# Products of zeros ahead of the first loads, and the first two weights' sums on VectorE with their late token blocks behind the next weights

## The chip, the cores and the metric

The kernel runs on one core of one Trainium2 chip. The core has a matrix engine (PE, with PEld for its weight loads), a vector engine (DVE), a scalar engine (ACT), GpSimd (POOL) and SyncE (SP), which here only issues DMA transfers. Sixteen DMA engines move data between HBM and the core's memory, SBUF; matrix products land in PSUM. The metric is the device time of one execution in microseconds. The time before is 1756.33 us, the median of three runs (1754.27 to 1756.72).

## The reference

One encoder layer for 1024 tokens of width 1024, with 16 learned meta tokens put in front. All arithmetic is float32. What the change touches is the very first step: the input projection of the normalised tokens, whose columns feed a retention branch, an attention branch and two gates.

```python
h = jnp.concatenate([meta, x], axis=1)
# per layer
u = _rmsnorm(h, norm_mix_w)
proj = u @ w_in
rq, rk, rv, rg, a_cq, a_ckv, a_kr, a_gret, a_gmla = jnp.split(proj, SPLIT_IDX, axis=-1)
y_ret = _head_group_norm(_bidir_retention(rq, rk, rv, decay_fwd, decay_bwd), gn_w)
y_ret = (silu(rg) * y_ret) @ w_ret_out
y_mla = _mla_attention(...) @ w_mla_out
h = h + (sigmoid(a_gret) * y_ret + sigmoid(a_gmla) * y_mla) @ w_o
h = h + (silu(u2 @ w_gate) * (u2 @ w_up)) @ w_down      # u2 = _rmsnorm(h, norm_ffn_w)
return _rmsnorm(h, norm_final_w)[:, N_META:]
```

## The kernel before

**Numbers in two halves.** PE multiplies operands of type float32r. A float32 tile is therefore split into a high half, a cast on ACT, and a low half, tile minus high half, on DVE (`split`, line 153; `bsplit` and `bscale`, lines 276 and 282, for token blocks, the latter with a factor per partition). Each product of two tiles is three matmuls: high by high, high by low, low by high.

**Seven products instead of eight.** A 256-column slice of a weight and the tokens are treated as 2 x 2 matrices of blocks. `seven` (line 184) loads the four blocks of a weight (a11, a21, a22, a12), forms sums of them (lines 192 to 194: s1 = a21 + a22, s2 = s1 - a11, a21 - a11, and later on line 210 s2 - a12), and returns `prod(b)`, which splits one of the seven sides and multiplies it with the token block of the same name. The names are 11, t2, t3, n1, 21, t4 and 22 (lines 30 and 31); in each of them four token blocks of 128 x 512 (q = 0 to 3) are summed, so one name is 12 matmuls. `seven_out` and `rest_out` combine the products into four output quarters; `rest_out` (line 303) takes one or more weights and goes through the names stage by stage: t2 of each, n1 of each, t3, t4, 22.

**The start** (lines 325 to 422). Products 11 and 21 of the first NP = 7 weights need no sums. For the first four weights the loop at line 356 loads x and the weight in turn (`xload`, line 328; `wfirst`, line 336: load, then split), scales and splits the token block, and multiplies what is there. Three more weights follow (line 377), then the seven banks are copied to SBUF (line 383) and the token blocks "21" are made, then the seven weights' blocks 21 (line 387) are multiplied. All these matmuls are on line 344: 7 x 2 x 12 = 168. Between them `second(q)` (line 366) loads the other token half and makes the blocks n1 and t2. Lines 399 to 408 load the meta tokens and place them in two tiles, `um` and `umd`, whose unused columns are zero (a memset on POOL). Lines 410 to 420 make the token blocks t3, then t4 and 22. Line 421 runs the five remaining names of the first two weights as one group: 2 x 5 x 12 = 120 matmuls, on line 220. Lines 657 to 665 go on with the third and fourth weight, sums of squares of the reloaded tokens (`squares`), and the value weights.

**Buffers.** Raw weights of `wfirst` and of `seven(w7, ...)` rotate through 5 buffers (`wr1`), high and low halves through 3 each (`wh1`, `wl1`). The second weight of the first group uses other pools: `wb` (3 buffers) for its raw blocks and `wf` (2 buffers) for its sums. PSUM has two pools of four banks, `pm` and `pc`; banks 0 to 3 of the start are in `pm`, 4 to 6 in `pc`. The pools `xp`, `wf` and `wb` are closed at the end of the `with` block; the rotary tables (`cosf`, `sinf`) and the reloaded tokens (`xl`) take their place in memory, so their loads wait until the old tiles have been read.

**Order.** Engines run their own queues in order and wait for each other by semaphores. The order within each queue is planned at compile time from a simulated run: an instruction that comes earlier in the program goes first where several are ready, but a later one can pass one that is not. `tc.issue_after(ins)` puts what is traced inside it behind `ins` on that engine. DMA loads and stores are issued by SP (`load` and `store`, lines 76 and 77), also in order: a transfer that waits for a buffer holds the ones behind it.

Of the kernel before, what the change touches and what calls it, by code (L numbers as in the profile page):

```python
# [11 lines left out]
AF = mybir.ActivationFunctionType  # L12
# [5 lines left out]
P = 128  # L18
# [21 lines left out]
NP = 7  # L40

# [7 lines left out]
def build(nc, tc, A, out):  # L49
# [29 lines left out]
    def f(t):  # L79
        return t.bitcast(F32)  # L80
# [4 lines left out]
    warm = mk(cp, (P, 1), "warm")  # L85
    pool.memset(warm, 0.0)
    act.activation(warm, warm, AF.Exp)
# [9 lines left out]
    load(cols, A["cols"])  # L97
# [86 lines left out]
    def seven(pools, srcs, blocks, meta=None):  # L184
        wr, ws, wh_, wl_, pm_ = pools
        nq = len(blocks)
# [5 lines left out]
        pool.tensor_add(s1, a21, a22)  # L192
        pool.tensor_sub(s2, s1, a11)  # L193
        pool.tensor_sub(a21, a21, a11)
# [3 lines left out]
        def prod(b, qs=range(nq)):  # L198
# [9 lines left out]
            if b not in w:  # L208
                if b == "22":
                    pool.tensor_sub(s2, s2, a12)  # L210
                hi, low = slot(wh_, F32R)[:, :n], slot(wl_, F32R)[:, :n]
                act.copy(hi, side[b])  # L212
                dve.tensor_sub(low, side[b], f(hi))  # L213
                w[b] = hi, low
# [40 lines left out]
    with ExitStack() as c1:  # L255
# [13 lines left out]
        umd = mk(mp, (P, 4, 48), "umd", F32R)  # L269
        places = [bta]  # L270
# [32 lines left out]
        def rest_out(group, pl):  # L303
            for prod, e, post in group:
                dve.tensor_add(e, prod("t2"), e)
            vs = [slot(pl) for _ in group]
            for (prod, e, post), v in zip(group, vs):
                dve.tensor_sub(v, e, prod("n1"))
            for (prod, e, post), v in zip(group, vs):
                dve.tensor_add(v, prod("t3"), v)  # L310
                post("22", v)
            for prod, e, post in group:
                t = slot(pl)
                dve.tensor_add(t, prod("t4"), e)
                post("21", t)
            for prod, e, post in group:
                dve.tensor_sub(e, e, prod("22"))
                post("12", e)
# [6 lines left out]
        with ExitStack() as c2:  # L325
# [9 lines left out]

            def wfirst(src, ph, plo):
                raw = slot(wr1)
                load(raw, src)
                return split(raw, ph, plo)
# [13 lines left out]

            banks = [mk(pm if i < 4 else pc, (P, 512), "mm") for i in range(NP)]
            x11, x21, wa11, es = [], [], [], []
            for i in range(4):
                x11.append(xload(2 * i, 0))
                wa11.append(wfirst(win(i)[0], wf if i == 3 else wh1, wf if i == 3 else wl1))
# [46 lines left out]
            for dst, src in ((um, xm), (umd, xd)):  # L405
                pool.memset(f(dst), 0.0)
# [3 lines left out]
            with tc.issue_after(made[0].ins), tc.issue_after(made[1].ins):  # L410
                for q in range(4):
                    dve.scalar_tensor_tensor(x12[q], x12[q], col(2 * q), x22[q], ALU.mult, ALU.subtract)
                    hi, lo = U[q]["t3"] = block("t3")
                    made[:] = act.copy(hi, x12[q]), dve.tensor_sub(lo, x12[q], f(hi))
            with tc.issue_after(made[0].ins), tc.issue_after(made[1].ins):
                for q in range(4):
                    dve.scalar_tensor_tensor(x21[q], x21[q], col(2 * q + 1), x11[q], ALU.mult, ALU.subtract)
                    U[q]["t4"] = bsplit("t4", x21[q])
                for q in range(4):
                    U[q]["22"] = bsplit("22", x22[q])  # L420
            rest_out([(seven(w7, win(0), U), es[0], rg_post(0)),
                      (seven((wb, wf, wh1, wl1, pc), win(1), U), es[1], rg_post(1))], cr)
# [1146 lines left out]
```

## Time and profile before

| | us |
|---|---|
| median of three runs | 1756.33 |
| the profiled execution | 1753.05 |
| its span (first to last instruction) | 1751.1 |
| busy in the first 100 us: PE, DVE, ACT, POOL | 89.44, 81.62, 56.66, 38.94 |
| granted TensorE clock over the span, as a share of full speed | 0.991 |

The profile is of one execution. A row of a timeline has the start and the length in microseconds from the span's start, the engine, the line of the kernel, the operation, what it writes and reads by the program's names, shapes and count; in brackets stands how long the engine was idle before and which instruction released it. Rows of SPq are the issuing of a transfer, not the transfer. A row of the windows has the stretch, then its length, then the busy time (and the number of instructions) of PE, PEld, DVE, ACT and POOL, the granted PE clock, the share of time in which the 16 DMA engines were busy, and the rate in GB/s. Matmuls overlap, so their distance is read from the starts, not from their lengths. A few matmul records can be missing.

### The profile page before, as it was taken

To read this page: it belongs to the slowest core of one execution; us is meant where nothing else is said; L and a number is where in the kernel's file an instruction comes from. 1 tells how busy PE (TensorE), PEld (TensorE's weight loads), DVE (VectorE), ACT (ScalarE), POOL (GpSimd) and SP (SyncE) were. 2 spreads that over 40 slices of the span, in tenths; PEclk is the share of its full clock that TensorE was granted. 3 is DMA by queue.
4 is the path that set the end of the run, shared out by engine and by line. 5 is a ranking of instruction groups with operands and counts; after the bars stand their busy time and mean duration, and the time that the engine had idled before them with its cause. 6 is when DMAs were issued, how large, how long until landed. Compare 5 with 4: busy or idle time off the path is not lost. (4 is left out here: it accounts for less than half of the span.)

```text
span 1751.1 us, 26268 instructions
## 1 busy us (share of the span) xinstructions
PE 1698.3 (97%) x8644; PEld 1427.5 (82%) x8644; DVE 1346.8 (77%) x2461; ACT 852.2 (49%) x1597; POOL 763.6 (44%) x585
## 2 busy tenths in 40 slices
PE   8999999999999999999999999999999999999998
PEld 6787677888887778999898888788888888788787
DVE  7846778888789876888888768776778887866775
ACT  7426566344424624778787346433333333522335
POOL 2450267575653421324322501566676666523431
PEclk9999999999999999999999999999999999999999
DMA  7876924566546875111122844233344445876612
GB/s 261 290 250 207 296 85 131 164 211 212 193 150 226 254 280 178 30 45 30 30 64 69 272 150 162 80 108 115 129 142 144 139 138 167 273 269 226 231 61 97
DMA packets 169913, 287.15 MB, mean 164 GB/s; under 512 B 20841, under 2 KB 46882, under 8 KB 169778
## 3 DMA queue, kind: packets, MB, share of 16 engines
q1 hardware_dynamic: 168626, 284.44, 48.8%
q8 instruction: 68, 1.11, 0.3%
q10 hardware_dynamic: 1152, 1.05, 0.2%
q14 instruction: 67, 0.55, 0.1%
HBM read 193.28 MB, written 92.06 MB: 163 GB/s over the span
## 5 line engine op out<-in xcount | busy, mean ns | idle before, releaser
L220 PE MATMUL mm<-slot,slot 128*128 128x512 f32 x2604 | 595.0, 390 | 3.6 <-DVE slot L213 1.9
L220 PEld LDWEIGHTS mm<-slot,slot 128*128 128x128 f32 x2604 | 487.3, 188 | 110.2 <-DVE slot L213 4.1
L212 ACT CAST slot<-slot 128x512 fp32r<-128x512 f32 (+1 forms) x385 | 226.8, 596 | 432.2 <-PE mm L220 339.5
L213 DVE TENSOR_TENSOR slot<-slot,slot 128x512 fp32r<-128x512 f32 (+1 forms) x385 | 350.2, 912 | 67.8 <-ACT slot L212 66.9
L192 POOL TENSOR_TENSOR slot<-slot,slot 128x512 f32<-128x512 f32 (+1 forms) x57 | 78.7, 1381 | 329.5 <-DMA slot<-in_w_in 116.5
L220 PE MATMUL mm<-ht,slot 128*128 128x512 f32 x552 | 184.2, 397 | 1.9 <-DVE slot L213 1.9
L220 PE MATMUL mm<-h,slot 128*128 128x512 f32 x440 | 153.2, 408 | 5.8 <-ACT slot L212 2.8
L210 POOL TENSOR_TENSOR slot<-slot,slot 128x512 f32<-128x512 f32 (+1 forms) x57 | 76.5, 1343 | 140.8 <-DVE slot L213 97.6
L155 DVE TENSOR_TENSOR slot<-slot,slot 128x512 fp32r<-128x512 f32 x123 | 97.1, 806 | 40.4 <-ACT slot L155 36.2
L220 PEld LDWEIGHTS mm<-ht,slot 128*128 128x128 f32 x552 | 103.1, 188 | 23.8 <-DVE slot L213 2.7
L155 ACT CAST slot<-slot 128x512 fp32r<-128x512 f32 x123 | 74.5, 618 | 76.7 <-POOL slot L1275 23.4
L1092 DVE TENSOR_SCALAR_CACHE_REDUCE pr<-s,sq_c 128x384 f32<-128x384 f32 (+1 forms) x192 | 103.3, 572 | 7.9 <-PE t L1110 5.3
L220 PE MATMUL mm<-lt,slot 128*128 128x512 f32 x276 | 108.6, 394 | 0.0
L220 PEld LDWEIGHTS mm<-h,slot 128*128 128x128 f32 x440 | 84.2, 193 | 26.3 <-ACT slot L212 5.3
L140 PE MATMUL mm<-slot,slot 128*128 128x512 f32 (+1 forms) x288 | 105.4, 366 | 0.0
L141 PE MATMUL mm<-slot,slot 128*128 128x512 f32 (+1 forms) x288 | 105.3, 366 | 0.0
L139 PE MATMUL mm<-slot,slot 128*128 128x512 f32 (+1 forms) x288 | 105.2, 367 | 0.0
L193 POOL TENSOR_TENSOR slot<-slot,slot 128x512 f32<-128x512 f32 (+1 forms) x57 | 83.4, 1463 | 48.6 <-DVE slot L213 42.3
L1105 DVE TENSOR_TENSOR ptl<-t,pth 128x512 fp32r<-128x512 f32 x128 | 85.7, 684 | 17.7 <-ACT pth L1104 17.2
L1136 POOL TENSOR_TENSOR oa<-oa,ob 64x256 f32<-64x256 f32 x32 | 24.0, 749 | 151.8 <-ACT ob L1135 151.8
L220 PE MATMUL mm<-l,slot 128*128 128x512 f32 x220 | 88.6, 404 | 0.0
L1104 ACT CAST pth<-t 128x512 fp32r<-128x512 f32 x128 | 71.8, 579 | 25.2 <-PE t L1102 24.8
(409 smaller groups left out, 3667.6 us busy)
## 6 DMA issues: line engine op xcount, KB each, us to landing
slot<-in_w_in SPq DMA_DIRECT2D x90, 256.0 KB
f_d<-slot SPq DMA_DIRECT2D x71, 256.0 KB
slot<-f_d SPq DMA_DIRECT2D x71, 256.0 KB
slot<-in_xT SPq DMA_DIRECT2D x48, 256.0 KB
slot<-z_d SPq DMA_DIRECT2D x44, 256.0 KB
slot<-in_w_g SPq DMA_DIRECT2D x44, 256.0 KB
slot<-in_w_u SPq DMA_DIRECT2D x44, 256.0 KB
fl_d<-slot SPq DMA_DIRECT2D x42, 256.0 KB
```

The costliest lines, as they stand in the source:

```text
L139: pe.matmul(ps, sh, mh, start=start, stop=False)
L140: pe.matmul(ps, sh, ml, start=False, stop=False)
L141: pe.matmul(ps, sl, mh, start=False, stop=stop)
L155: split.done = act.copy(hi, t), dve.tensor_sub(lo, t, f(hi))
L192: pool.tensor_add(s1, a21, a22)
L193: pool.tensor_sub(s2, s1, a11)
L210: pool.tensor_sub(s2, s2, a12)
L212: act.copy(hi, side[b])
L213: dve.tensor_sub(low, side[b], f(hi))
L220: pe.matmul(ps, sw[:, ks], sx, start=begins and q == qs[0] and i == 0, stop=q == nq - 1 and i == 2, skip_group_check=True)
L1092: dve.tensor_scalar(pr[:, c], ps[:, :n], sq_c[:, qb : qb + 1], None, ALU.mult, ALU.max, accum_out=mx[:, j : j + 1])
L1105: dve.tensor_sub(pt[1][d], tp, f(pt[0])[d])
```

## The change

- Thirteen matmuls (`NIDLE`) of the zero tiles, 384 columns each, are put ahead of the first real product, into a PSUM bank that nothing reads. For this the zeroing of `um` and `umd` moves from line 406 to where the tiles are made, and from POOL to DVE.
- The table of per-channel factors (`cols`) and the first raw weight are loaded by DMAs that ACT issues. The dummy exponential (which makes ACT load its table) moves behind them.
- The two weights of the first group do their sums (six at once, two later) on DVE instead of POOL, by the new argument `adds`. Later weights stay on POOL.
- The two weights change places in the group.
- The making of t3, and of t4 and 22, moves into `rest_out`, between the t2 stage and the n1 stage. The second of them is issued behind the last split of the t2 stage: `split.done` is now also set in `prod`.

```diff
--- before.py
+++ after.py
@@ -39,6 +39,8 @@
 
 NP = 7
 
+NIDLE = 13
+
 O_AT = ((6, 1), (6, 2), (6, 3), (7, 0), (7, 1), (7, 2))
 
 
@@ -82,9 +84,6 @@
 
     cp = sb(top, "const")
     dram = sb(top, "scratch", space=DRAM)
-    warm = mk(cp, (P, 1), "warm")
-    pool.memset(warm, 0.0)
-    act.activation(warm, warm, AF.Exp)
     ident = mk(cp, (P, P), "ident")
     make_identity(nc, ident)
     ones = mk(cp, (P, 1), "ones")
@@ -94,7 +93,9 @@
     gneps_c = mk(cp, (P, 1), "gneps")
     pool.memset(gneps_c, GN_EPS)
     cols = mk(cp, (P, NCOL), "cols")
-    load(cols, A["cols"])
+    nc.scalar.dma_start(cols, A["cols"])
+    warm = mk(cp, (P, 1), "warm")
+    pool.memset(warm, 0.0)
     rstd = mk(cp, (P, NB + 1), "rstd")
     rst2 = mk(cp, (P, NB + 1), "rst2")
     sq_c = mk(cp, (P, NB + 1), "sq_c")
@@ -181,17 +182,18 @@
 
 
 
-    def seven(pools, srcs, blocks, meta=None):
+    def seven(pools, srcs, blocks, meta=None, adds=None):
         wr, ws, wh_, wl_, pm_ = pools
+        adds = adds or pool
         nq = len(blocks)
         n = nq * P
         a11, a21, a22, a12 = [slot(wr)[:, :n] for _ in range(4)]
         for i, t in enumerate((a11, a21, a22, a12)):
             load(t, srcs[i])
         s1, s2 = [slot(ws)[:, :n] for _ in range(2)]
-        pool.tensor_add(s1, a21, a22)
-        pool.tensor_sub(s2, s1, a11)
-        pool.tensor_sub(a21, a21, a11)
+        adds.tensor_add(s1, a21, a22)
+        adds.tensor_sub(s2, s1, a11)
+        adds.tensor_sub(a21, a21, a11)
         side = {"11": a11, "t2": s2, "t3": a21, "n1": s1, "21": a12, "t4": a22, "22": s2}
         banks, w, begun, done = {}, {}, [], set()
 
@@ -207,10 +209,9 @@
                 return ps
             if b not in w:
                 if b == "22":
-                    pool.tensor_sub(s2, s2, a12)
+                    adds.tensor_sub(s2, s2, a12)
                 hi, low = slot(wh_, F32R)[:, :n], slot(wl_, F32R)[:, :n]
-                act.copy(hi, side[b])
-                dve.tensor_sub(low, side[b], f(hi))
+                split.done = act.copy(hi, side[b]), dve.tensor_sub(low, side[b], f(hi))
                 w[b] = hi, low
             wh, wl = w[b]
             for q in qs:
@@ -267,6 +268,8 @@
         w7 = (wr1, ws1, wh1, wl1, pm)
         um = mk(mp, (P, KT, 48), "um", F32R)
         umd = mk(mp, (P, 4, 48), "umd", F32R)
+        for t in (um, umd):
+            dve.memset(f(t), 0.0)
         places = [bta]
 
         def block(nm):
@@ -300,9 +303,12 @@
                 store(rg_d[2 * j + int(name[0]) - 1, :, half(name)], side_copy(name, t))
             return post
 
-        def rest_out(group, pl):
+        def rest_out(group, pl, late=None):
+            late = late or ()
             for prod, e, post in group:
                 dve.tensor_add(e, prod("t2"), e)
+            for make in late:
+                make()
             vs = [slot(pl) for _ in group]
             for (prod, e, post), v in zip(group, vs):
                 dve.tensor_sub(v, e, prod("n1"))
@@ -333,10 +339,13 @@
             def col(k):
                 return column(C_MIX + k)
 
+            def wraw(src, begin=load):
+                raw = slot(wr1)
+                begin(raw, src)
+                return raw
+
             def wfirst(src, ph, plo):
-                raw = slot(wr1)
-                load(raw, src)
-                return split(raw, ph, plo)
+                return split(wraw(src), ph, plo)
 
             def products(ps, w, b, q, begins):
                 ks = slice(q * P, q * P + P)
@@ -351,11 +360,20 @@
                     return rg_post(i)
                 return lambda name, t: store(g_d[2 * (i - 4) + int(name[0]) - 1, :, half(name)], side_copy(name, t))
 
+
+            idle = mk(pc, (P, 512), "mm")
+            for i in range(NIDLE):
+                pe.matmul(idle[:, : KT * 48], um.rearrange("p a b -> p (a b)")[:, :P], um.rearrange("p a b -> p (a b)"),
+                          start=True, stop=True)
             banks = [mk(pm if i < 4 else pc, (P, 512), "mm") for i in range(NP)]
             x11, x21, wa11, es = [], [], [], []
+            raw = wraw(win(0)[0], nc.scalar.dma_start)
+            act.activation(warm, warm, AF.Exp)
             for i in range(4):
                 x11.append(xload(2 * i, 0))
-                wa11.append(wfirst(win(i)[0], wf if i == 3 else wh1, wf if i == 3 else wl1))
+                if i:
+                    raw = wraw(win(i)[0])
+                wa11.append(split(raw, wf if i == 3 else wh1, wf if i == 3 else wl1))
                 U[i]["11"] = bscale("11", x11[i], col(2 * i))
                 for q in range(i):
                     products(banks[i], wa11[i], "11", q, q == 0)
@@ -403,23 +421,27 @@
             x4 = xm.rearrange("p (q a) t -> p q a t", a=2)
             dve.tensor_sub(xd, x4[:, :, 1, :], x4[:, :, 0, :])
             for dst, src in ((um, xm), (umd, xd)):
-                pool.memset(f(dst), 0.0)
                 act.copy(dst[:, :, 0:NM], src)
                 dve.tensor_sub(dst[:, :, 32:48], src, f(dst)[:, :, 0:NM])
 
-            with tc.issue_after(made[0].ins), tc.issue_after(made[1].ins):
-                for q in range(4):
-                    dve.scalar_tensor_tensor(x12[q], x12[q], col(2 * q), x22[q], ALU.mult, ALU.subtract)
-                    hi, lo = U[q]["t3"] = block("t3")
-                    made[:] = act.copy(hi, x12[q]), dve.tensor_sub(lo, x12[q], f(hi))
-            with tc.issue_after(made[0].ins), tc.issue_after(made[1].ins):
-                for q in range(4):
-                    dve.scalar_tensor_tensor(x21[q], x21[q], col(2 * q + 1), x11[q], ALU.mult, ALU.subtract)
-                    U[q]["t4"] = bsplit("t4", x21[q])
-                for q in range(4):
-                    U[q]["22"] = bsplit("22", x22[q])
-            rest_out([(seven(w7, win(0), U), es[0], rg_post(0)),
-                      (seven((wb, wf, wh1, wl1, pc), win(1), U), es[1], rg_post(1))], cr)
+
+
+            def make_t3():
+                with tc.issue_after(made[0].ins), tc.issue_after(made[1].ins):
+                    for q in range(4):
+                        dve.scalar_tensor_tensor(x12[q], x12[q], col(2 * q), x22[q], ALU.mult, ALU.subtract)
+                        U[q]["t3"] = bsplit("t3", x12[q])
+
+            def make_t4():
+                with tc.issue_after(split.done[0].ins), tc.issue_after(split.done[1].ins):
+                    for q in range(4):
+                        dve.scalar_tensor_tensor(x21[q], x21[q], col(2 * q + 1), x11[q], ALU.mult, ALU.subtract)
+                        U[q]["t4"] = bsplit("t4", x21[q])
+                    for q in range(4):
+                        U[q]["22"] = bsplit("22", x22[q])
+
+            rest_out([(seven((wb, wf, wh1, wl1, pc), win(1), U, adds=dve), es[1], rg_post(1)),
+                      (seven(w7, win(0), U, adds=dve), es[0], rg_post(0))], cr, (make_t3, make_t4))
         mf = sb(mid, "factor", 1, side="right")
 
         small, sums = sb(mid, "small", 8, side="right"), sb(mid, "sums", 2, side="right")
```

## The prediction

> **What bounds the kernel now.** I read the page's head first, then a table of busy time by stretch, then the timelines of PE, DVE, POOL and SP over the stretch where PE falls behind.
>
> ```profile
> span 1751.1 us, 26268 instructions
> PE 1698.3 (97%) x8644; PEld 1427.5 (82%) x8644; DVE 1346.8 (77%) x2461; ACT 852.2 (49%) x1597; POOL 763.6 (44%) x585
> ```
>
> PE is busy for 97% of the span, so only 53 us of idle PE can be won anywhere, plus the time in which PE runs slowly. The windows (time, then busy time and instructions of each engine, granted clock, DMA share, GB/s) say where.
>
> ```profile
> core 0: us, PE busy (x) PEld busy (x) DVE busy (x) ACT busy (x) POOL busy (x), PEclk, DMA share, GB/s
> 5.00:10.00 5.00, 4.13 (x9) 2.78 (x10) 3.73 (x6) 3.61 (x7) 0.00 (x0) 1.00 1.00 330
> 10.00:20.00 10.00, 10.00 (x45) 8.22 (x44) 7.50 (x12) 7.63 (x14) 0.00 (x0) 1.00 1.05 392
> 20.00:30.00 10.00, 10.00 (x46) 8.29 (x45) 9.71 (x11) 8.78 (x16) 4.97 (x3) 1.00 0.73 259
> 30.00:40.00 10.00, 9.65 (x43) 7.67 (x42) 10.00 (x17) 7.32 (x14) 0.00 (x0) 1.00 0.61 191
> 40.00:55.00 15.00, 10.66 (x40) 8.06 (x39) 13.83 (x18) 7.67 (x16) 6.86 (x5) 0.89 0.47 153
> 55.00:81.00 26.00, 26.00 (x117) 21.53 (x116) 22.95 (x38) 15.35 (x30) 6.81 (x6) 1.00 0.96 327
> 81.00:105.00 24.00, 24.00 (x108) 19.88 (x107) 17.50 (x18) 5.28 (x9) 23.69 (x16) 1.00 0.96 331
> 140.00:190.00 50.00, 45.45 (x201) 34.47 (x200) 33.84 (x70) 35.16 (x70) 0.00 (x0) 1.00 0.72 233
> ```
>
> From 20 to 55 us DVE is the full engine, not PE. From 55 to 105 PE never idles. The rows of PE that mark the losses (start, length, engine, line, idle before and releaser):
>
> ```profile
> 5.69 0.80 PE L344 MATMUL mm<-h,slot 128*128 128x512 f32 x1 [5.69 <-ACT slot L155]
> ...
> 7.97 0.80 PE L344 MATMUL mm<-h,slot 128*128 128x512 f32 x1 [0.18 <-ACT slot L155]
> ...
> 10.64 0.40 PE L344 MATMUL mm<-l,slot 128*128 128x512 f32 x1
> ...
> 30.86 0.39 PE L344 MATMUL mm<-l,slot 128*128 128x512 f32 x1
> 31.60 0.72 PE L344 MATMUL mm<-h,slot 128*128 128x512 f32 x2 [0.35 <-DVE slot L155]
> ...
> 42.52 0.40 PE L344 MATMUL mm<-l,slot 128*128 128x512 f32 x1
> 47.26 0.73 PE L344 MATMUL mm<-h,slot 128*128 128x512 f32 x2 [4.34 <-DVE slot L155]
> ...
> 51.43 0.44 PE L220 MATMUL mm<-lt,slot 128*128 128x512 f32 x1
> ...
> 54.45 0.62 PE L220 MATMUL mm<-ht,slot 128*128 128x512 f32 x2
> ...
> 80.74 0.39 PE L220 MATMUL mm<-ht,slot 128*128 128x512 f32 x1
> ```
>
> The first pair's five stages are 5 x 24 = 120 products; four of them run early, so 116 start from 54.45 to 80.74, one every 0.2266 us. The 168 products of L344 and these 120 would take 288 x 0.2266 = 65.3 us at that pace; they take 80.74 - 5.69 = 75.05. **9.8 us are lost**, in four places. From 5.69 to 10.64 ten products start, worth 2.27 us, in 4.95: 2.7 lost. At 31.60: 31.60 - 30.86 - 0.23 = 0.5. At 47.26: 47.26 - 42.52 - 0.23 = 4.5. After that gap eleven products start from 47.26 to 51.43, worth 2.5 us, in 4.17: 1.7 lost, and the granted clock of 40 to 55 us is 0.89. About 0.4 us is left over.
>
> DVE's rows say why PE waits at 31.60 and 47.26 (both for the low half of a weight, L155), and POOL's rows beside them why DVE is late:
>
> ```profile
> 17.37 0.68 DVE L370 TENSOR_TENSOR slot<-slot,slot 128x512 f32<-128x512 f32 x1
> ...
> 24.42 1.79 DVE L373 SCALAR_TENSOR_TENSOR slot<-slot,cols,slot 128x512 f32<-128x512 f32 x1
> 26.13 1.79 DVE L285 SCALAR_TENSOR_TENSOR ln<-slot,cols,hn 128x512 fp32r<-128x512 f32 x1
> 27.84 1.78 DVE L375 TENSOR_TENSOR lt<-slot,ht 128x512 fp32r<-128x512 f32 x1
> 29.54 0.74 DVE L373 SCALAR_TENSOR_TENSOR slot<-slot,cols,slot 128x512 f32<-128x512 f32 x1
> ...
> 35.14 2.72 DVE L412 SCALAR_TENSOR_TENSOR slot<-slot,cols,slot 128x512 f32<-128x512 f32 x4
> 37.79 0.68 DVE L155 TENSOR_TENSOR slot<-slot,slot 128x512 fp32r<-128x512 f32 x1
> 38.39 2.48 DVE L414 TENSOR_TENSOR lt<-slot,ht 128x512 fp32r<-128x512 f32 x4
> 40.80 5.81 DVE L417 SCALAR_TENSOR_TENSOR slot<-slot,cols,slot 128x512 f32<-128x512 f32 x4
> 46.53 0.68 DVE L155 TENSOR_TENSOR slot<-slot,slot 128x512 fp32r<-128x512 f32 x1
> ```
>
> ```profile
> 24.02 1.64 POOL L192 TENSOR_TENSOR slot<-slot,slot 128x512 f32<-128x512 f32 x1 [21.93 <-DVE ln L285]
> ...
> 41.41 1.29 POOL L192 TENSOR_TENSOR slot<-slot,slot 128x512 f32<-128x512 f32 x1 [12.35 <-DMA slot<-in_w_in]
> ```
>
> The thirteenth weight's low half (46.53) stands behind the four L417 of the t4 blocks, and those take 1.45 us each instead of L412's 0.68 while POOL adds.
>
> **The change part by part.** *Order and engine of the sums.* Six sums (three for each of two weights) go from POOL to DVE, and two L210 later. A two-input DVE operation on this tile takes 0.68 us, with starts 0.60 apart in a chain: 6 x 0.60 = 3.6 us added before the stages, 1.2 within them. Taken off DVE: (1.79 + 1.79 + 1.78) - (0.74 + 0.74 + 0.68) = 3.2 us at 24 to 30, and 5.81 - 2.72 = 3.1 us at 41 to 46. So DVE has about 1.5 us less to do in sum, although it gets eight more instructions. The eight t3 operations (2.72 + 2.48 = 5.2 us) may fill in as now, but the twelve of t4 and 22 (about 7.6 us at 0.60 to 0.68) stand behind the next weights' splits.
>
> Does DVE make the deadlines? In the code, from the first L370 (17.37) to the last weight's low half, 25 operations must run: four each of L285 and L373 at 0.68, and nine L155, four L370, four L375 at 0.60: 15.6 us, so 33.0. With the sums 36.6, with t3 41.8. PE without stalls starts at 5.69 - 0.45 + 0.1 = 5.34, keeps 1.4 us of its first losses (both below), and ends its 168 products at 5.34 + 1.4 + 38.1 = 44.8; its thirteenth weight starts at 39.4, its fourteenth at 42.1. t3 is last in the program among these, so the weights' halves can pass it: I cost the stalls at 31.60 and 47.26 as gone, **0.5 + 4.5**, and with the gap the slow products, **1.7**. What is late next is t4, needed 72 products, 16.3 us, after 44.8: by then DVE has t4 itself (4 x 0.68 + 4 x 0.60 = 5.1), eight weight halves and six sums off the banks (14 x 0.60 = 8.4): 13.5 of 16.3. If all of t3 were left over too, 5.2 - 2.8 = 2.4 us would be lost. I take 0.
>
> The second group's sums wait for a load that starts late:
>
> ```profile
> 38.49 0.33 SPq L190 DMA_DIRECT2D slot<-in_w_in  x1
> ```
>
> It is issued when the twelfth raw weight is released by DVE (38.39) and POOL's sum starts 2.9 us later (41.41). On DVE this wait would hold everything behind it, the t2 halves and t3 to 22, for up to 2.9 us. It costs PE nothing while DVE is that far ahead: without L412 the twelfth half is done by 33.0, the wait ends at 36, before 39.4.
>
> *Start.* The zero products need only the two memsets, now on DVE; POOL's take 0.42 and 0.26:
>
> ```profile
> 1.18 0.42 SPq L330 DMA_DIRECT2D slot<-in_xT  x1
> 1.48 0.42 POOL L406 MEMSET um<- 128x384 f32 x1
> 1.65 0.42 SPq L338 DMA_DIRECT2D slot<-in_w_in  x1
> 4.41 0.72 ACT L284 ACTIVATE h<-slot,cols 128x512 fp32r<-128x512 f32 x1 [2.18 <-DMA slot<-in_xT]
> ```
>
> So PE can start near 1.2. From 7.97 to 10.64 six products start, 0.445 apart; 13 zero products of 384 columns at that pace, scaled by 384/512, take 13 x 0.33 = 4.3 us and end near 5.5, which delays the first real one by 0 to 0.3 us (I take 0.1). If PE is at full pace by 7.97, those six take 1.36 instead of 2.67: **1.3 won**. The four products before 7.97 wait for data (1.4 us of the 2.7 stays). With `cols` on ACT's queue SP issues x at 0.73 instead of 1.18: **0.45**. Below: 0, since DMA share is already 1.00 from 5 us; above: 0.92, both issues off SP. I take 0.45, as the first transfer sets when data starts to flow. ACT issues both at 0.43 each, then loads its table: done near 3.1, before x lands near 4.0.
>
> The second queue might also add bandwidth. The row 10 to 20 us has 1.05 and 392 GB/s with one queue. The Trainium skill, "DMA: Bandwidth & Descriptors", section "Issuing engines are not separate DMA queues", says that all queues run on the same 16 engines and only issue time is saved; by it this term is 0.45 to 0.92, by the other view more. The share of 1.00 agrees with the page.
>
> **Sum** at the end of the first pair: 4.5 + 1.7 + 0.5 + 1.3 + 0.45 - 0.1 = **8.4 us** (0 to 9.8 + 0.45). Behind it PE is full to 140 us, so what it gains is kept only if its feeders come earlier too. From 55 to 105 us DMA is at 0.96 and POOL at 23.69 of 24 us after 81; and the engines' orders are planned at compile time, so every later order may shift (four products of L220 before the last weight's show such a plan). From 140 to 190 PE idles 4.55 us among waits for ACT and DVE, which may grow or shrink. I take 1.9 us given back (bounds -3 to 8.4, the nearest rows being that 4.55 and the gain itself): **6.5 us net**.
>
> The profiled execution took 1753.05 (its span 1751.1 and 1.95 around it), so 1746.5 by its own time. It lies 3.3 below the median of the runs, 1756.33; a median after it should come out 6.5 below that: **1749.8**.
>
> **The rivals.** *Given back.* POOL's order and DMA's rate between 55 and 105 don't follow: bulk loads (the reloaded tokens, the value weights) keep their time, and the third and fourth weights' sums on POOL wait as now. For: DMA 0.96, POOL full. Against: PE never waited there, so there is slack that no row measures. Net 2.5 us: 1753.8. Chance 0.2.
>
> *Slower: SP is blocked by the late blocks.* The tiles that hold the tokens' raw halves are reused by the tables and token reloads:
>
> ```profile
> 52.55 0.68 DVE L279 TENSOR_TENSOR lt<-slot,ht 128x512 fp32r<-128x512 f32 x1
> ...
> 57.36 2.33 SPq L459 DMA_DIRECT2D slot<-in_xT  x5
> ```
>
> The last 22 block is now made at 52.55 and the reload starts at 57.36. If t4 and 22 slip to just before their use (44.8 + 96 x 0.2266 = 66.6), the reload starts near 67, 9.6 us later, and on SP, whose order is fixed, the next weights' loads wait behind it. PE, though early, then waits for a DMA-bound stretch that ends up to 9.6 us later than now; how much slack it has there no row shows (0 to 9.6), so I take the middle: 4.8 us above, 1761. It decides once the last 22 block is later than about 60 us. Against: DVE should have it by 54. Chance 0.1.
>
> *The zero products do nothing for PE's pace.* Then 1.3 goes: 5.2 net, 1751.1. Chance 0.1. For it: the six products at 0.445 come 2.3 us after the first real one, so pace lags work by microseconds. The Trainium skill, "TensorE: Matmul & The Clock Gate", Part 1, has a half-rate clock until a free-running window of about 3.4 us was busy. By that rule 4.3 us of products may straddle two windows, and warmth comes 3.4 to 6.8 us after 1.2, before or near 7.97. The pace in the rows agrees, though the granted clock shows 1.00 at 5 to 10 us.
>
> **How the numbers follow.** The forecast has 0.6. About 0.2%, 3.5 us, is what a measurement of this kernel can tell from no change. Faster: 0.57 of the forecast, 0.08 of the third rival, 0.05 of the first = 0.70. Slower by as much: nearly all of the second = 0.09. Within: 0.21. The range: below, 8.4 + 3 off the median, 1745; above, the first rival with nearly all given back, 1757.
>
> **What would show it.** Right: PE's first L344 near 5.3 at 0.23 spacing from 8 us; no idle over 0.5 us and clock 1.00 from 31 to 55; L344 over by 45 to 46; the third weight's first product near 72.4 instead of 80.74; DVE's operations at 0.6 to 0.75 us before 55. Wrong: an idle PE between 45 and 72 waiting for t4 or 22; SP's L459 later than 60; waits for POOL's L193 or loads at 72 to 105; or new table loads at 140 to 190.

## Result and profile after

| | before | after |
|---|---|---|
| median, us | 1754.43 (8 runs, 1751.34 to 1756.72) | 1745.24 (8 runs, 1740.51 to 1751.19) |
| ratio of the times | | 0.9948, 95% interval 0.9932 to 0.9964 |
| profiled execution, us | 1753.05 | 1740.51 |
| its span, us | 1751.1 | 1738.7 |
| third weight's first product, us | 80.74 | 73.05 |

The changed kernel is faster by 9.2 us (interval 6.3 to 11.9). 1749.8 was predicted, with 1745 to 1757 as the range, so the median lies 0.24 above the range's lower end. The profiled execution after is the fastest of its eight; that has to be kept in mind below.

Three numbers carry the comparison. **M** is the start of the third weight's first product, where the prediction closes its sum. The **gain at M** is what happened up to the end of the first pair. The **rest**, span minus M, is everything behind it. Before: M 80.74, rest 1670.4. After: M 73.05, rest 1665.7. So 7.7 us of the profiles' 12.4 come from the first pair, and 4.7 from behind it.

The head of the page, after:

```profile
span 1738.7 us, 26295 instructions
PE 1694.5 (97%) x8657; PEld 1424.9 (82%) x8657; DVE 1349.6 (78%) x2471; ACT 851.2 (49%) x1597; POOL 746.1 (43%) x575
```

PE's busy time fell by 3.8 us, although 13 products of zeros were added; the other 8.6 of the 12.4 us were idle PE. The windows after, in the same stretches and with the same columns as before:

```profile
20.00:30.00 10.00, 10.00 (x46) 8.28 (x45) 9.90 (x17) 10.00 (x20) 0.00 (x0) 1.00 0.75 251
30.00:40.00 10.00, 10.00 (x46) 8.29 (x45) 10.00 (x17) 6.45 (x12) 0.00 (x0) 1.00 0.81 269
40.00:55.00 15.00, 14.52 (x65) 11.72 (x64) 14.54 (x26) 9.59 (x19) 0.69 (x1) 1.00 0.62 206
55.00:81.00 26.00, 26.00 (x116) 21.47 (x116) 24.13 (x37) 14.04 (x25) 8.13 (x7) 1.00 0.93 326
140.00:190.00 50.00, 45.76 (x202) 35.16 (x202) 34.52 (x59) 34.58 (x65) 1.49 (x1) 1.00 0.82 264
```

From 40 to 55 us PE is busy for 14.52 us instead of 10.66, 65 matmuls start instead of 40, and the granted clock is 1.00 instead of 0.89. DVE is as full as before, but it does 26 operations in that stretch instead of 18. From 140 to 190 us PE's idle time is 4.24 us, before 4.55.

PE's rows after (start, length, idle before and releaser in brackets):

```profile
1.32 4.46 PE L366 MATMUL mm<-um 128*128 128x384 f32 x13 [1.32 <-DVE um L272]
6.52 0.50 PE L353 MATMUL mm<-h,slot 128*128 128x512 f32 x1 [0.74 <-ACT slot L156]
...
44.83 0.39 PE L353 MATMUL mm<-h,slot 128*128 128x512 f32 x1
45.05 0.39 PE L221 MATMUL mm<-ht,slot 128*128 128x512 f32 x1
...
54.77 0.50 PE L221 MATMUL mm<-ht,slot 128*128 128x512 f32 x1 [0.48 <-ACT slot L214]
...
73.05 0.39 PE L221 MATMUL mm<-ht,slot 128*128 128x512 f32 x1
```

L353 is before's L344, L221 its L220. The gaps at 31.60 and 47.26 are gone; the 168 products of the start end at 45.05. One wait is left before M, 0.48 us at 54.77. But the first real product comes at 6.52, later than before's 5.69. ACT's rows say why:

```profile
0.73 0.42 ACTq L96 DMA_DIRECT2D cols<-in_cols  x1
...
4.34 0.72 ACT L287 ACTIVATE h<-slot,cols 128x512 fp32r<-128x512 f32 x1 [1.19 <-DMA cols<-in_cols]
5.23 0.72 ACT L287 ACTIVATE h<-slot,cols 128x512 fp32r<-128x512 f32 x1 [0.17 <-DMA slot<-in_xT]
5.86 0.60 ACT L156 CAST slot<-slot 128x512 fp32r<-128x512 f32 x1
```

The factors, now issued by ACT at 0.73, are what the first scaling waits for until 4.34. Then the plan puts the second token block's scaling (5.23) ahead of the first weight's cast (5.86), which the first product needs.

DVE's rows after:

```profile
26.66 0.69 DVE L196 TENSOR_TENSOR slot<-slot,slot 128x512 f32<-128x512 f32 x1
...
32.86 2.74 DVE L432 SCALAR_TENSOR_TENSOR slot<-slot,cols,slot 128x512 f32<-128x512 f32 x4
35.51 0.69 DVE L156 TENSOR_TENSOR slot<-slot,slot 128x512 fp32r<-128x512 f32 x1
...
39.12 0.69 DVE L156 TENSOR_TENSOR slot<-slot,slot 128x512 fp32r<-128x512 f32 x1
39.73 0.69 DVE L194 TENSOR_TENSOR slot<-slot,slot 128x512 f32<-128x512 f32 x1
...
44.07 2.73 DVE L438 SCALAR_TENSOR_TENSOR slot<-slot,cols,slot 128x512 f32<-128x512 f32 x4
...
51.74 1.89 DVE L282 TENSOR_TENSOR lt<-slot,ht 128x512 fp32r<-128x512 f32 x3
```

The last (fourteenth) weight's low half (L156) is at 39.12; before, the thirteenth's was at 46.53 and the last one at 49.54. The sums (L194 to L196) take 0.69 each. The four t4 operations (L438, before L417) stand behind the weights at 44.07 and take 2.73 instead of 5.81. The last 22 block is done by 53.6.

### The profile page after: what moved, and what is told of

It is laid out like the page before. It is cut to its first block, busy times and chain, and to the rows that moved or that the text cites. A ratio compares the mean times of both kernels' runs of the same rounds, so it can differ in the third digit from the quotient of the medians.

```text
span 1738.7 us, 26295 instructions
## 1 busy us (share of the span) xinstructions
PE 1694.5 (97%) x8657; PEld 1424.9 (82%) x8657; DVE 1349.6 (78%) x2471; ACT 851.2 (49%) x1597; POOL 746.1 (43%) x575
## 4 chain that ended last, share of the span: by engine, by line
PE 66%; DVE 9%; DMA 5%; ACT 3%; issue 2%; POOL 1%; SPq 0%; DVEq 0%; ACTq 0%; POOLq 0%
PE mm L221 42%; PE o L1153 3%; PE mm L140 3%; PE mm L141 3%; PE mm L142 3%; PE t L1124 2%; PE s L140 1%; DVE slot L156 1%; PE s L142 1%; PE s L141 1%; DMA slot<-g_d 1%; PE mm L740 1%; DVE ptl L1127 1%; DVE slot L214 1%; PE mm L765 1%
## 5 line engine op out<-in xcount | busy, mean ns | idle before, releaser
L221 PE MATMUL mm<-slot,slot 128*128 128x512 f32 x2604 | 595.4, 390 | 3.7 <-DVE slot L214 1.9
L221 PEld LDWEIGHTS mm<-slot,slot 128*128 128x128 f32 x2604 | 487.2, 188 | 110.7 <-DVE slot L214 4.4
L214 ACT CAST slot<-slot 128x512 fp32r<-128x512 f32 (+1 forms) x385 | 226.7, 596 | 424.9 <-PE mm L221 340.0
L214 DVE TENSOR_TENSOR slot<-slot,slot 128x512 fp32r<-128x512 f32 (+1 forms) x385 | 352.0, 917 | 65.2 <-ACT slot L214 64.1
L194 POOL TENSOR_TENSOR slot<-slot,slot 128x512 f32<-128x512 f32 (+1 forms) x55 | 72.7, 1323 | 346.3 <-DMA slot<-in_w_in 79.6
L221 PE MATMUL mm<-ht,slot 128*128 128x512 f32 x552 | 184.0, 396 | 2.9 <-DVE slot L214 1.9
L221 PE MATMUL mm<-h,slot 128*128 128x512 f32 x440 | 151.8, 405 | 4.3 <-DVE slot L214 2.7
L156 DVE TENSOR_TENSOR slot<-slot,slot 128x512 fp32r<-128x512 f32 x123 | 100.3, 833 | 37.1 <-ACT slot L156 33.7
L212 POOL TENSOR_TENSOR slot<-slot,slot 128x512 f32<-128x512 f32 (+1 forms) x55 | 72.3, 1314 | 128.0 <-DVE slot L214 82.0
L221 PEld LDWEIGHTS mm<-ht,slot 128*128 128x128 f32 x552 | 102.8, 188 | 25.6 <-DVE slot L214 3.0
L156 ACT CAST slot<-slot 128x512 fp32r<-128x512 f32 x123 | 74.4, 619 | 76.0 <-PE mm L590 22.4
L221 PE MATMUL mm<-lt,slot 128*128 128x512 f32 x276 | 108.5, 393 | 0.0
L221 PEld LDWEIGHTS mm<-h,slot 128*128 128x128 f32 x440 | 83.4, 191 | 24.5 <-DVE slot L214 4.8
L195 POOL TENSOR_TENSOR slot<-slot,slot 128x512 f32<-128x512 f32 (+1 forms) x55 | 81.3, 1478 | 51.7 <-DVE slot L214 46.3
L221 PE MATMUL mm<-l,slot 128*128 128x512 f32 x220 | 87.8, 400 | 0.0
```

Source lines behind the costliest of these rows:

```text
L156: split.done = act.copy(hi, t), dve.tensor_sub(lo, t, f(hi))
L194: adds.tensor_add(s1, a21, a22)
L195: adds.tensor_sub(s2, s1, a11)
L212: adds.tensor_sub(s2, s2, a12)
L214: split.done = act.copy(hi, side[b]), dve.tensor_sub(low, side[b], f(hi))
L221: pe.matmul(ps, sw[:, ks], sx, start=begins and q == qs[0] and i == 0, stop=q == nq - 1 and i == 2, skip_group_check=True)
```

## Experiments

The theory: the gain at M is the group's part of the change (sums on DVE, late token blocks), which takes DVE's slow operations and the t4 blocks out of the weights' way; the start adds its own gain, mostly by the products of zeros; what lies behind M is chance. Rivals: the later 4.7 us are a second effect of the change; the sums or the order alone do all of it; the two parts need each other. All kernels but *before_again* and *zerosalone* are made from the changed one.

**Both kernels once more.** No edit, for the size of chance.

> The changed kernel, unaltered. Milestone M is the start of the third weight's first product (80.74 us before, 73.05 after); the rest is the span less M (1670.4 before, 1665.7 after). Theory A: the change acts before M alone, the other 4.7 us of the profiled runs' difference are chance from run to run. Then M comes out at 72.5 to 73.6 and the rest anywhere from 1665 to 1673. Rival B: the change also shortens the rest; then the rest is 1665 to 1667 again and that of the kernel before 1669.5 to 1671.5.

> The kernel before, unaltered, for a second trace. Theory A: M 80.2 to 81.3, and a rest (span less M) that lies among those of the changed kernel, 1665 to 1673. Rival B: a rest of 1669.5 to 1671.5, at least 3 us above the changed kernel's.

The third weight's first product of the two, each from PE's timeline of its kernel:

```profile
73.97 0.39 PE L221 MATMUL mm<-ht,slot 128*128 128x512 f32 x1
```

```profile
81.52 0.39 PE L220 MATMUL mm<-ht,slot 128*128 128x512 f32 x1
```

The changed kernel: 1748.09 us (4 runs) beside 1755.51, ratio 0.9954 (0.9939 to 0.9968); span 1747.1, so the rest is 1673.1, against 1665.7 in its first profile. The kernel before: span 1752.0, rest 1670.5 against 1670.4. The same program's rest differs by 7.4 us from one execution to the next, so the 4.7 us behind M are no effect that needs a cause. Both new M lie a little above theory A's ranges (73.97 over 73.6, 81.52 over 81.3), which were too narrow. M repeats within 0.9 us, and is the finer measure here; from now on runs are compared by it. Each of the other kernels has one trace, so a difference in M of less than about 0.9 us can't be told from chance. Mean before: 81.13. The traces of *noswap*, *startnoswap*, *groupand* and *zerosalone* come from another chip than those of the other experiments, on which neither kernel was traced again; the nearest comparison is *noswap*, whose M (73.66) lies between the changed kernel's two.

**Without the products of zeros.** The bank, the loop and its 13 matmuls are left out.

```diff
-            idle = mk(pc, (P, 512), "mm")
-            for i in range(NIDLE):
-                pe.matmul(idle[:, : KT * 48], ...
```

> The changed kernel without its 13 products of zeros (and without the PSUM tile that they write). Theory: they bring PE to full pace by the first real product; without them the first ten products come about 0.44 us apart as before, the first real product stays near 6.5 us, and M is 0.6 to 1.6 us later than 73.05: 73.7 to 74.7. Rival: PE waits for data then anyway, so the zeros are worth nothing: M 72.8 to 73.3. Second rival: the zeros delay the first real product; M 72.2 to 72.8.

M 76.23 (1751.58 us): 2.3 to 3.2 later than the changed kernel, more than the theory allowed. The first real product came at 7.36, and the products stood 0.43 apart until past 12 us. This is pace and a later first product together; *groupand* below takes them apart.

**The first loads on SP.** `cols` and the first weight are issued by SP again, the dummy exponential comes first; the rest as changed.

```diff
-    nc.scalar.dma_start(cols, A["cols"])
+    load(cols, A["cols"])
...
+    act.activation(warm, warm, AF.Exp)
...
-            raw = wraw(win(0)[0], nc.scalar.dma_start)
-            act.activation(warm, warm, AF.Exp)
```

> The changed kernel with the factors and the first weight loaded by SP in the order of before, and the dummy exponential first again. Theory: the first real product came at 6.52 us instead of 5.69 because the factors landed at 4.34 over ACT's queue and the plan put the second token block's scaling (0.63 us) ahead of the first weight's cast on ACT; with SP's loads it comes at 5.6 to 5.9 and M is 0.5 to 1.0 us earlier than 73.05: 72.0 to 72.6. Rival, as the forecast had it: the loads on ACT's queue are worth 0.45 us and the late start has another cause; then M is 73.0 to 73.6.

The time is 1746.95, ratio 0.9951 (0.9934 to 0.9967); M 73.18, within the changed kernel's own spread. The first product did come earlier, at 5.74, but nothing of that was left at M. ACT's timeline of this kernel and then PE's show two later waits:

```profile
8.19 0.72 ACT L288 ACTIVATE h<-slot,cols 128x512 fp32r<-128x512 f32 x1 [1.16 <-DMA slot<-in_xT]
```

```profile
29.59 0.50 PE L354 MATMUL mm<-h,slot 128*128 128x512 f32 x1 [0.24 <-ACT slot L157]
```

Here the third token block is waited for until 8.19; in the changed kernel it is scaled at 7.30 without a wait (at 7.85 in *again*). So the loads on ACT's queue make the first product later and a later block earlier. By the windows of the start's products, 27 start from 5 to 12.5 us here and 25 in the changed kernel; both have 148 by 40 us. The rest of the lead went at 29.59, where PE waits for the cast of a weight on ACT (busy for 10.00 of the 10 us from 20 to 30). The range of M was the rival's, its reason (another cause of the late first product) was not: the cause was right, and cost nothing.

**Sums back on POOL.**

```diff
-            rest_out([(seven((wb, wf, wh1, wl1, pc), win(1), U, adds=dve), es[1], rg_post(1)),
-                      (seven(w7, win(0), U, adds=dve), es[0], rg_post(0))], cr, (make_t3, make_t4))
+            rest_out([(seven((wb, wf, wh1, wl1, pc), win(1), U), es[1], rg_post(1)),
+                      (seven(w7, win(0), U), es[0], rg_post(0))], cr, (make_t3, make_t4))
```

> The changed kernel with the first two weights' sums back on POOL; the late blocks stay behind the t2 weights. M is the start of the third weight's first product (73.05 and 73.97 us in the two traces of the changed kernel, 80.74 and 81.52 in those of before). Theory: the gap before the thirteenth weight was made by the order of DVE's queue, POOL's sums only lengthen single operations; DVE's operations of 1.79 us come back beside the sums, PE waits 0.3 to 1.5 us for low halves near 30 us, no gap near 42; M 73.3 to 75.5. Rival: POOL's slowing of DVE made the gap; a gap of over 3 us comes back and M is 77 to 81.

M 76.13 (1751.57 us), between the theory's range and the rival's: the sums' engine is worth 2.2 to 3.1 us beside the rest of the change. No gap comes back near 47; the wait has moved behind the start, to a weight half of the group. PE's rows with a wait after 10 us:

```profile
27.33 0.74 PE L353 MATMUL mm<-h,slot 128*128 128x512 f32 x2 [0.22 <-DVE slot L156]
...
54.61 0.73 PE L221 MATMUL mm<-hn,slot 128*128 128x512 f32 x2 [1.33 <-DVE slot L214]
...
57.82 0.74 PE L221 MATMUL mm<-hn,slot 128*128 128x512 f32 x2 [0.18 <-DVE slot L214]
```

DVE's slow operations are back too: 1.79, 1.78 and 1.77 at 23.79 to 28.9 and 4.81 for the four L438, while POOL adds.

**Token blocks ahead of the group again,** sums on DVE and places swapped as changed.

```diff
+            make_t3()
+            with tc.issue_after(made[0].ins), tc.issue_after(made[1].ins):
+                for q in range(4):
+                    dve.scalar_tensor_tensor(x21[q], x21[q], col(2 * q + 1), x11[q], ALU.mult, ALU.subtract)
+                    U[q]["t4"] = bsplit("t4", x21[q])
+                for q in range(4):
+                    U[q]["22"] = bsplit("22", x22[q])
...
-                      (seven(w7, win(0), U, adds=dve), es[0], rg_post(0))], cr, (make_t3, make_t4))
+                      (seven(w7, win(0), U, adds=dve), es[0], rg_post(0))], cr)
```

> The changed kernel with the t3, t4 and 22 blocks made ahead of the group as before; the sums stay on DVE. Theory (order of the queue): four t4 products and four of their low halves, some 5 us, stand ahead of the twelfth weight's low half, which is done near 41.3 instead of 36.2 while PE needs it near 37.1: one gap of 3 to 5 us there, with slow products after it if it is over 3.4 us; M 77 to 80. Rival (contention): without POOL's sums DVE keeps up; gap under 1.5 us, M 73 to 75.

M 77.62 (1748.53 us), in the theory's range, but with two short gaps in place of one long: the order is worth about 4 us. PE's rows:

```profile
39.92 0.50 PE L353 MATMUL mm<-h,slot 128*128 128x512 f32 x1 [1.23 <-ACT slot L156]
...
42.18 0.73 PE L353 MATMUL mm<-h,slot 128*128 128x512 f32 x2 [1.52 <-DVE slot L156]
...
66.62 0.47 PE L221 MATMUL mm<-ht,slot 128*128 128x512 f32 x1 [1.02 <-ACT mm L493]
```

Two of the three waits are for the last weights' halves behind t3 and t4, as in the kernel before but shorter, since DVE's operations take 0.69 here, and with no slow products after them. The third, for the sums of squares, may have to do with the swapped places; that wasn't tried.

**The start alone on the old group.** Sums on POOL and blocks ahead, that is the edits of the last two together; zeros and ACT's loads stay. *start_only* keeps the swapped places, *startnoswap* puts them back.

> Of the change only the start (zeros, loads on ACT's queue) and the swapped places of the two weights: sums on POOL, blocks ahead of the group. Theory: PE then waits for DVE's queue near 40 us whatever it won at the start, so the start's gain is swallowed: one gap of 6 to 9 us, M 79.5 to 82.5, as before the change. Rival (the parts add up): the start's 2 us stay, M 78.0 to 79.2.

> As start_only (sums on POOL, all token blocks ahead of the group, the changed start kept) but with the two weights in their old places. Start_only gave M 85.76, 4 to 5 us later than before. Theory (the swap is what made start_only worse than before: the second weight's sums wait for a load that comes late): M 79 to 82, that is before's 80.74 to 81.52 less at most 2. Rival (an earlier start on the old group loses its gain by itself, because DVE and POOL, not PE, set the pace from 24 us on): M 84 to 87.

*start_only*: M 85.76, 1764.18 us, worse than before and outside what either theory said. *startnoswap*: M 81.02, 1754.73 us, no different from before. So swapped places cost 4.7 us on the old group. PE's waits of *start_only* that the other doesn't have lie at 66.05, 70.08 and 74.76 (0.82, 0.99 and 2.12 us, the last for the sums of squares on ACT); why the swap brings them is not settled. With the old places the start gives nothing at all: PE is ahead until 27 us, and then waits. PE's rows of *startnoswap*:

```profile
27.28 0.73 PE L353 MATMUL mm<-h,slot 128*128 128x512 f32 x2 [0.72 <-DVE slot L156]
...
38.76 0.50 PE L353 MATMUL mm<-h,slot 128*128 128x512 f32 x1 [2.26 <-ACT slot L156]
...
41.62 1.22 PE L353 MATMUL mm<-h,slot 128*128 128x512 f32 x2 [2.13 <-DVE slot L156]
```

**The places swapped back** in the changed kernel, nothing else.

```diff
-            rest_out([(seven((wb, wf, wh1, wl1, pc), win(1), U, adds=dve), es[1], rg_post(1)),
-                      (seven(w7, win(0), U, adds=dve), es[0], rg_post(0))], cr, (make_t3, make_t4))
+            rest_out([(seven(w7, win(0), U, adds=dve), es[0], rg_post(0)),
+                      (seven((wb, wf, wh1, wl1, pc), win(1), U, adds=dve), es[1], rg_post(1))], cr, (make_t3, make_t4))
```

> The changed kernel with only the first pair's two weights put back into their old places (the one with the 5-buffer pool first). M is the start of the third weight's first product; the changed kernel has shown 73.05 and 73.97. Theory (the swap does nothing, since both weights' sums are ready long before their use): M 73.0 to 74.2, DVE's sums in starts 0.60 apart, no idle PE over 0.7 us between 31 and 55. Rival (the swap is what lets the late token blocks fit, because the weight with its own buffers can be loaded first): M 75 or more, with idle PE between 40 and 60 that waits for a sum or a weight half of the first pair.

M 73.66 (1748.35 us), between the changed kernel's two. With the sums on DVE and the blocks late, the swap does nothing.

**The group's part alone.** *sp_loads* without the products of zeros: the start is the old one.

> The group's part of the change alone: sums on DVE, late token blocks, swapped places; no products of zeros, cols and first weight loaded by SP, dummy exponential first. Theory (the start is worth what no_zeros lost, 2.3 to 3.2 us, and the loads on ACT's queue nothing): M 75.3 to 77, PE's slow spacing of 0.43 until past 10 us, time 0.997 to 1.000 of before. Rival (what no_zeros lost came from the ACT-queue loads left without their cover, so that the group alone gives nearly everything): M 73 to 74.5, time 0.994 to 0.996 of before.

M 75.18; 1750.56 us (10 runs) beside 1757.66, ratio 0.9958 (0.9945 to 0.9970). M lies 0.1 below the theory's range and the ratio in the rival's; the intervals of the times can't tell 1.7 us, so M decides: the group alone gives 81.13 - 75.18 = 5.95 us. The four traces with both the zeros and the group's part (73.05 and 73.97 of the changed kernel, 73.18 of *sp_loads*, 73.66 of *noswap*) have a mean M of 73.47: the start adds 1.7. Of what *no_zeros* lost, 76.23 - 75.18 = 1.05 would belong to ACT's loads without their cover (first product at 7.36 there, at 5.90 here), which is hardly more than two executions differ by.

**The zeros alone,** added to the kernel before.

```diff
+        for t in (um, umd):
+            dve.memset(f(t), 0.0)
...
+            idle = mk(pc, (P, 512), "mm")
+            for i in range(13):
+                pe.matmul(idle[:, : KT * 48], ...
...
-                pool.memset(f(dst), 0.0)
```

> Before with only the 13 products of zeros added (the two tiles are zeroed on DVE for it). Before showed M 80.74 and 81.52. Theory (the pace gained at the start is swallowed by the stretch from 24 to 47 us, in which DVE is the full engine): M 80.2 to 82, with a gap of 4 us or more near 47 and fewer slow products before 11 us. Rival (the gain adds up with the rest): M 77.8 to 79.5, the gap near 47 no longer than 4.4.

M 81.75 (1757.9 us): no gain. The windows of the start's matmuls alone (PE's count is the second number) show where it went; first the kernel before, then this one, then the changed one:

```profile
5.00:12.50 7.50, 6.63 (x19) 4.79 (x20) 1.00 1.02 354
12.50:40.00 27.50, 27.15 (x120) 22.17 (x119) 1.00 0.77 269
```

```profile
5.00:12.50 7.50, 6.42 (x25) 4.98 (x26) 1.00 1.01 373
12.50:40.00 27.50, 25.83 (x113) 20.77 (x112) 1.00 0.78 273
```

```profile
5.00:12.50 7.50, 5.94 (x25) 4.62 (x26) 1.00 1.02 373
12.50:40.00 27.50, 27.50 (x123) 22.78 (x122) 1.00 0.84 290
```

With the zeros six products more start by 12.5 us, in both kernels. On the old group seven fewer start from there to 40 us, and the sum is 138 against 139: the lead is lost. On the new group it is kept, 148. PE's rows of *zerosalone* show the waits for weight halves, two on DVE and one on ACT:

```profile
30.95 0.73 PE L346 MATMUL mm<-h,slot 128*128 128x512 f32 x2 [1.53 <-DVE slot L155]
...
45.51 0.80 PE L220 MATMUL mm<-ht,slot 128*128 128x512 f32 x1 [2.49 <-ACT slot L212]
...
49.03 1.22 PE L346 MATMUL mm<-h,slot 128*128 128x512 f32 x2 [2.30 <-DVE slot L155]
```

**Twice as many zeros.** `NIDLE = 26` instead of 13.

> The changed kernel with 26 products of zeros instead of 13. The first 13 took 4.46 us, 0.343 each. Theory: another 13 end at 8.0 to 10.2 us and hold the first real product up to then; data for 24 products is there by 12.4, so PE is behind by 0.8 to 3 us afterwards: M 74.2 to 76.5. Rival: early on PE only waits for data, so the later start is caught up: M 73.0 to 74.0.

M 77.95 (1748.94 us), later than expected. PE's rows:

```profile
1.32 6.72 PE L366 MATMUL mm<-um 128*128 128x384 f32 x26 [1.32 <-DVE um L272]
7.88 0.39 PE L353 MATMUL mm<-h,slot 128*128 128x512 f32 x1
...
20.73 0.50 PE L353 MATMUL mm<-h,slot 128*128 128x512 f32 x1 [1.80 <-ACT slot L156]
...
23.54 1.06 PE L353 MATMUL mm<-h,slot 128*128 128x512 f32 x2
24.39 0.63 PE L353 MATMUL mm<-l,slot 128*128 128x512 f32 x1
```

The 26 took 6.72 us against 4.46 for 13, so the second half took 2.26. The first real product was 0.7 to 1.4 us later by it than in the changed kernel's two profiles. The greater loss is a new wait at 20.73 (ACT's order is another one here) with slow products behind it to about 26 us; the granted clock from 20 to 30 us is 0.83.

## Why the prediction was right, and where it wasn't

**The stalls, 4.5 + 1.7 + 0.5 = 6.7.** Right in mechanism and nearly in size. No wait is left from 31 to 54 us and the clock there is 1.00. The group's part alone gives 5.95; the new wait at 54.77 (0.48, and a slower restart: 54.77 - 53.89 - 0.23 = 0.65 us lost) is nearly all of the difference to 6.7, though two executions differ by as much. The prediction costed what is late next at nothing and looked for it at t4 and 22; it is a cast of a weight half on ACT (L214), and all kernels with both parts of the group's change but *zeros_26*, which is behind by then, show it with 0.48. ACT's row shows that the cast itself stood idle for PE:

```profile
54.09 0.62 ACT L214 CAST slot<-slot 128x512 fp32r<-128x512 f32 x1 [2.95 <-PE mm L221]
```

What it can want of PE is one of the three buffers for high halves (`wh1`), which PE still read; no run here has a fourth. DVE's deadline sum held: the last weight's half was due by 42.1 and came at 39.12. Both halves of the reason are needed: undoing the sums costs 2.7 against the mean M of 73.47, undoing the order 4.2, undoing both (old places) 7.6, which is all.

**DVE's operations back to 0.6 to 0.75 us.** Right: 0.69 with the sums on DVE, 1.77 to 1.79 again in *pool_sums* and *zerosalone*, always beside POOL's sums. It can also be POOL that gets longer: in *startnoswap* DVE's operations from 45.70 to 48.19 keep 0.68, and POOL's first sum beside them (L194 at 45.81) takes 3.52 instead of 1.3. The Trainium skill, "SBUF — State Buffer", section "Who interferes with whom", has a DVE instruction with two SBUF inputs contend with a GpSimd instruction that reads SBUF; the rows agree.

**The start, 1.3 + 0.45 - 0.1 = 1.65.** The sum came out (1.7 measured), but one of its terms was wrong, so that it fits so well is luck in part. The **0.45 for loads on ACT's queue** is wrong: the first product comes at 6.52 or 7.22 instead of 5.34, for the factors land at 4.34, and it doesn't matter, for with the loads on SP the first product is at 5.74 and M the same. What the prediction missed is that the first product doesn't set the pace here: *sp_loads* lost its 0.8 us by 40 us, in part to a later token block and for the rest to a cast on ACT. The **1.3 for the pace** held in kind: with the loads on SP the zeros are worth 75.18 - 73.18 = 2.0. The slow pace lasts to 11.26 or longer in *groupand*, whose first product is at 5.90, and to 10.64 in the kernel before; a difference of 0.7 is also within chance.

**That the terms add up** is the step that the prediction took for granted and that held only for this set of edits. On the old group the start is worth 0.1 (*startnoswap* 81.02, before 81.13) and the zeros alone -0.6 (81.75), both nothing beside what two executions differ by. On the new group the start is worth 1.7. The prediction had read the reason off the windows itself (DVE, not PE, is the full engine from 20 to 55 us), but didn't draw from it that an earlier PE would only wait longer there.

**The end of the first pair.** 72.4 was predicted for M; 73.05 and 73.97 were measured, a gain of 7.6 on the means (81.13 - 73.51) instead of 8.4. The 0.8 is no more than two executions differ by; the wait at 54.77 (0.65) and the late first product are what the rows show of it.

**1.9 given back behind it.** Too much. In the first two profiles the lead is 7.7 at M and still 7.55 at the last product of this line, first before, then after:

```profile
523.14 0.39 PE L742 MATMUL mm<-v,slot 128*128 128x128 f32 x2
```

```profile
515.59 0.39 PE L764 MATMUL mm<-v,slot 128*128 128x128 f32 x2
```

In the second two (*before_again*, then *again*) it is 7.55 at M and 6.54 there:

```profile
524.72 0.39 PE L742 MATMUL mm<-v,slot 128*128 128x128 f32 x2
```

```profile
518.18 0.39 PE L764 MATMUL mm<-v,slot 128*128 128x128 f32 x2
```

So 0.1 and 1.0 were given back, and the second can be chance: it goes between 140 and 190 us, where PE idles 5.13 us in *again* and 4.41 in *before_again*, and 4.24 in the changed kernel's first profile. The medians differ by 9.2 and, in the second set of runs, by 7.4, about as much as the 7.6 at M. The fear was that the planned orders of all later work would shift. They didn't: in the first two profiles PE, DVE, ACT and POOL each take their instructions in the same order in both kernels from 100 us on, and SP its transfers from 125 us on.

**The size.** 6.5 was forecast, 7.6 at M, 7.4 to 9.2 in the times: up to +1.9 for what wasn't given back, -0.8 at M, and chance of the size that *again* shows. That 1745.24 lies so near the lower end of the range is in part such chance: the second set of the changed kernel's runs has 1748.09. The kernel before, too, came out 1.9 lower with eight runs (1754.43) than with the three that the forecast starts from.

**The rivals.** *Given back* fell: in both profiles of the changed kernel PE has no wait for loads or POOL's sums from 56 to 105 us. *SP blocked by the late blocks* fell at its own condition: the last 22 block is done by 53.6, not beyond 60, and the reload starts earlier than before's 57.36. SP's row after:

```profile
51.17 3.29 SPq L481 DMA_DIRECT2D slot<-in_xT  x5
```

*The zeros do nothing* fell for the changed kernel; for the kernel before it would have had the gain right, but not the reason, since the pace did rise there (25 products by 12.5 us instead of 19). The kernel slower than before did turn up in the experiments (*start_only*), by another mechanism than the one that was weighed.

## What to carry to other kernels

Before summing the gains of edits, ask of each which engine is full behind it: a lead won at the start is lost at the next stretch in which another engine sets the pace, and is worth something only together with the edit that frees that engine. Where an engine's operations vary twofold in length, look first for what runs beside them, and then for what stands ahead of the operation that the waiting engine needs. When one execution's tail varies by 7 us, judge an early edit by a milestone inside the trace, not by the span.

## What the runs showed of the hardware

**A wait of 1.80 us can bring the slow pace back.** In *zeros_26* PE waits 1.80 us up to 20.73 and another 0.27 up to 21.73; from about 22.5 to 26 us the products start 0.43 apart, and the clock from 20 to 30 us is 0.83. The length of a wait alone doesn't decide: behind the 2.12 of *start_only* the products start at full pace:

```profile
74.76 0.47 PE L221 MATMUL mm<-ht,slot 128*128 128x512 f32 x1 [2.12 <-ACT mm L493]
75.07 0.39 PE L221 MATMUL mm<-lt,slot 128*128 128x512 f32 x1
75.30 0.63 PE L221 MATMUL mm<-ht,slot 128*128 128x512 f32 x2
```

Two waits of 1.23 and 1.52 us within 3.5 us in *early_blocks* did not bring the slow pace back (clock 1.00 from 40 to 55), 2.26 and 2.13 in *startnoswap* did (0.77). The Trainium skill, "TensorE: Matmul & The Clock Gate", Part 1, has the clock halve after at least one idle window of about 3.4 us; here less was enough in *zeros_26*, and 2.12 us was not in *start_only*.

**The slow pace of the start isn't in the granted clock.** It reads 1.00 from 5 to 10 us in every run, also where products stand 0.43 apart. The 13 zero products took 0.343 each (4.46 / 13), the next 13 took 0.174 (2.26 / 13): PE came to full pace about 4.5 us after its first product. In the kernel before, where that is a real one, it took 10.64 - 5.69 = 4.95, and in *groupand* at least 11.26 - 5.90 = 5.36.
